# A fifth chunk of seven-product blocks in a down projection, with a last stage that works by pairs of tiles

## The chip, the cores and the metric

The kernel runs on one core of a Trainium2 chip. The metric is the device time of one execution in microseconds (us); the median of three runs before the change is 2358.19 us (2357.68 to 2359.34). PE is TensorE (matrix products), DVE VectorE, ACT ScalarE, POOL GpSimd, SP SyncE, whose queue issues most transfers.

## The reference, cut to what matters

One encoder layer: a layer norm, a token mixer (a recurrence and an attention), a second norm, a gated feed-forward network with a short convolution, and a third norm. There are 544 tokens: 512 of a prompt and 32 of a running stream. The change lies in the last two lines, the down projection and the norm behind it.

```python
D_MODEL = 2048
D_FF = 5632
...
def conv_ffn(x, conv_buf, w_up, w_gate, conv_w, conv_b, w_down):
    T = x.shape[1]
    u = x @ w_up
    ext = jnp.concatenate([conv_buf.astype(u.dtype), u], axis=1)
    a = conv_b + sum(ext[:, j:j + T] * conv_w[j] for j in range(CONV_W))
    h = jax.nn.silu(a) * (x @ w_gate)
    return h @ w_down, ext[:, -(CONV_W - 1):]
...
        ff, conv_new = conv_ffn(h, conv_cache[l], w_ffn_up[l], w_ffn_gate[l], conv_w[l], conv_b[l], w_ffn_down[l])
        h = layer_norm(ALPHA * h + ff, ln2_g[l], ln2_b[l])
```

## The kernel before

Features lie on the 128 partitions, tokens along the free axis, in two halves of NI = 272 tokens (`H_[0]`, the first tokens, and `H_[1]`, the second). Every operand of a matmul is held as a rounded high part and a remainder, the low part, and each product is taken three times: high by high, high by low, low by high. A weight block of 128 x 1024 is loaded by SP into one of eight raw slots (`pump` takes the next of `pending` whenever a slot comes free; `release` frees one), ACT rounds it into `wh` (L1193) and DVE takes the remainder into `wl` (L1194). There are three buffers for each.

**Block products.** The up, gate and down projections use a scheme with seven products in place of eight for a 2 x 2 split of K, outputs and tokens. The products are named 11, s1, s2, s4, s3, 12, 22 (`ORDER`); s1, s2, s3 and 22 need a difference of weight blocks, which DVE forms in place (`Blocks.form`, L1186). One `Item` or `Twin` is one product: 24 matmuls of 128 x 272 into one PSUM bank. X banks take 11 and add s2, s3 and 22 to it; B banks take s1 and s4, and then 12. After each product `sink` adds a bank to the sum `y` in SBUF. `PLACE` says which quarter of y a product's bank belongs to: (output tile of a pair, half of the tokens). So s4 and 12 reach the first tokens only.

**Order.** `play` (from L1585) writes the engines' order out by hand. While PE multiplies item n, DVE adds the bank of item n-1, DVE and ACT split the weight of item n+2 (`prep`), and DVE forms the weight of item n+3. Smaller tasks wait in `fills`, each with a cost, and `drain` takes them in the room that an item leaves. `hooks` put transfers and other work behind named items. All of PE, DVE and ACT keep the order of the program.

**Down projection.** `CHUNKS` of four pairs of hidden tiles each go through block products: four chunks, 16 pairs, 32 K tiles (FD). A chunk has four rounds, one for each quarter q of the output tiles, and each round has the seven products. The operands of a chunk (sums and differences of hidden tiles, in two parts) are made in the up and gate stage (`gated`, from L1511: four sums and two `part`s for each pair below NS) and go through DRAM (`op_dr`). Of the pairs from NS on, `hid_dr` takes the plain hidden tiles.

**The K tiles that are left.** Twelve K tiles in three groups of four are taken plainly, by 8 pairs of output tiles c: `Whole` items for both halves of the tokens at once, one group for c = 4 to 7 and two for c = 0 to 3; then `last_half(1)` and `last_half(0)` take the rest for the second and the first tokens, pair by pair in the order `LAST`. `before_last` takes the second last group for c = 4 to 7, `last` the last one for all. In each half `Norm.first` finds a rough mean from the first pair, which is taken off everything that follows (`cb`): by GpSimd in the second tokens (`collect`, L2095), by a matmul in the first (`shift`, L2083). ACT squares each tile, DVE and GpSimd add up the sums s1 and s2. `Norm.stats` brings them across the partitions by matmuls, GpSimd takes the power -1/2, matmuls spread mean and scale. The second tokens are normalised tile by tile while the first tokens' products run (`scaled_last`, L2046 and L2047), and the first tokens at the very end (L2168, L2170, L2191 on DVE, L1133 and L1134 on GpSimd, L2037 on ACT), each tile stored by a transfer of its own (L2038).

Of the kernel before, what the change touches and what calls it, by code (L numbers as in the profile page):

```python
# [15 lines left out]
P = 128  # L16
D = 2048
# [30 lines left out]
CHUNKS = (4, 4, 4, 4)  # L48
# [11 lines left out]
def tile_encoder_step(ctx, tc, xp, xs, w_in, w_in4, w_kr, w_q_b, w_kv_b, w_out, w_up, w_gate, w_down, w_down2,  # L60
# [1560 lines left out]
    with tc.manual_schedule():  # L1621
# [190 lines left out]

        def down_items(g, q):
# [11 lines left out]
            def sink(name, x):  # L1825
                t, j = PLACE[name]
                ps = twin(banks[x])
                y = ysq[q].rearrange("p (c t) n -> p c t n", c=2)[:, :, t, H_[j]]
                if g == 0 and (t, j) not in fresh:
                    fresh.add((t, j))  # L1830
                    V.scalar_tensor_tensor(out=y, in0=y, scalar=ALPHA, in1=ps, op0=ALU.mult, op1=ALU.add)
                else:
                    V.tensor_tensor(out=y, in0=y, in1=ps, op=ALU.add)
# [9 lines left out]
        class Whole:  # L1843

            n, name = 8, "11"

            def __init__(self, c, g, tiles, first, last):
                self.c, self.k0, self.tiles, self.first, self.last = c, FD + 4 * g, tiles, first, last
                self.g, self.raw, self.time, self.sink = self, {}, 6.0, self.gather if last else None
                pending.append((self, "11", w_down2[g, c], 8))  # L1850

            def form(self):
                return 0.0

            def prep(self):
                self.w = [t.rearrange("p (k c) -> p k c", k=4) for t in rounded(self.raw["11"].t, 8)]
                release(self, "11")
                return 1.25

            def multiply(self):  # L1860
                if self.first:
                    self.tiles += [main_tile(), psA.tile([P, 1024], F32, name="acc", tag="acc")]
                for t in range(2):
                    for k in range(4):
                        mm3(both(self.tiles[t]), (self.w[0][:, k], self.w[1][:, k]), (t * P, t * P + P),
                            hid[self.k0 + k], self.first and k == 0, self.last and k == 3)

            def gather(self):
                for t in range(2):
                    y = ysq[self.c // 2][:, 2 * (self.c % 2) + t]  # L1870
                    V.tensor_tensor(out=y, in0=y, in1=hold(self.tiles[t]), op=ALU.add)
                return 1.5
# [6 lines left out]
        NG = (NF - FD) // 4  # L1879
        for c in (4, 5, 6, 7, 0, 1, 2, 3):  # L1880
            tiles, gs = [], range(NG - 2 if c >= 4 else NG - 1)
            items += [Whole(c, g, tiles, g == 0, g == gs[-1]) for g in gs]

# [11 lines left out]
        staged = {}  # L1895

        def stage_hid(g, name):
            t = staged[g] = home[name].tile([P, 4, T], F32, name=f"hx{g}", tag=f"op{name}0")
            G.dma_start(t, hid_dr[:, 4 * g:4 * g + 4])

        def split_group(g, i):
            for b, name in enumerate(("11", "12")):
                t = home[name].tile([P, 2, 2, T], R, name=f"hid{name}", tag=f"op{name}{i}")
                for f in range(2):
                    split_hid(FD + 4 * g + 2 * b + f, staged[g][:, 2 * b + f], t[:, f, 0], t[:, f, 1])
# [10 lines left out]
        L4 = (NW - NU) // len(CHUNKS)  # L1916
# [3 lines left out]
        n3 = NU + 3 * L4  # L1920
        at(n3 + 2, lambda: stage_hid(0, "s1"))
        at(n3 + 5, lambda: split_group(0, 0))
        at(n3 + 10, lambda: stage_hid(1, "s2"))
        at(NW, lambda: split_group(1, 1))
        at(NW - 8, lambda: retired.add(lt))

        ws9, ws10, tail = {}, {}, {}
# [5 lines left out]

        late9 = {c: Late(w_down2[NG - 2, c]) for c in (4,)}
        late10 = {c: Late(w_down2[NG - 1, c]) for c in (4, 5)}
        late9.update({c: Late(w_down2[NG - 2, c]) for c in range(5, 8)})

        def open_tail():
            x1_stack.close()
            free[:] = [s for s in free if s[0] is not lt]  # L1940
            tail["ap"] = ctx.enter_context(pool("ap2", bufs=KD))
            tail["hp2"] = ctx.enter_context(pool("hp2", "right"))
            tail["sps"], sp = stack(pool("sp", "right"))
            tail["hx"] = sp.tile([P, 4, T], F32, name="hx")
            G.dma_start(tail["hx"], hid_dr[:, 4 * NG - 4:])

        def split_tail_hid():
            for f in range(4):
                h, l = (tail["hp2"].tile([P, T], R, name=f"h{n}{f}") for n in "HL")
                split_hid(NF - 4 + f, tail["hx"][:, f], h, l)  # L1950

        def split_10(c, src):
            rv = src.rearrange("p (k c) -> p k c", k=4)
            for t in range(2):
                wh, wl = (tail["ap"].tile([P, 512], R, name=n, tag=n).rearrange("p (k c) -> p k c", k=4)
                          for n in ("aH", "aL"))
                A.activation(wh, rv[:, :, t * P:(t + 1) * P], AF.Copy)
                V.tensor_tensor(out=wl, in0=rv[:, :, t * P:(t + 1) * P], in1=wh.bitcast(F32), op=ALU.subtract)
                ws10[2 * c + t] = wh, wl

        def first_10(c):
            split_10(c, late10[c].raw["w"].t)
            release(late10[c], "w")

        def split_9(c):
            src = late9[c].raw["w"].t
            if c == 4:
                w = [p.tile([P, 8 * P], R, name=tag, tag=tag) for p, tag in (free.pop() for _ in range(2))]
                A.activation(w[0], src, AF.Copy)
                V.tensor_tensor(out=w[1], in0=src, in1=w[0].bitcast(F32), op=ALU.subtract)  # L1970
            else:
                w = rounded(src, 8)
            ws9[c] = [t.rearrange("p (k c) -> p k c", k=4) for t in w]
            release(late9[c], "w")

        at(NW + 3, open_tail)
        at(NW + 5, split_tail_hid)
        at(NW + 8, lambda: first_10(4))
        at(NW + 9, lambda: first_10(5))
        at(NW + 9, lambda: split_9(4))  # L1980
        at(NW + 10, lambda: split_9(5))
        at(NW + 11, lambda: split_9(6))

# [5 lines left out]
        split_9(7)  # L1989
        dma(conv_d, uc)  # L1990
        ys = [ysq[k // 4][:, k % 4] for k in range(KD)]
        tail["sps"].close()


    with pool("tl") as ff:
        LAST = (4, 5, 6, 0, 1, 2, 3, 7)

        def split_last(c):
            p, tag = free.pop(0)
            free.append((p, tag))  # L2000
            t = p.tile([P, 8 * P], F32, name=tag, tag=tag)
            dma(t, w_down2[NG - 1, c])
            split_10(c, t)

        split_last(6)
        split_last(0)
# [10 lines left out]

        turn = [0]

        def tail_tag(name):  # L2020
            turn[0] += 1
            return ("a", "ext")[turn[0] % 2], 2

        one_f = ff.tile([P, P], F32, name="one_f", tag="ext", bufs=2)
        ones_r = ff.tile([P, P], R, name="ones_r")
        V.memset(one_f, 1.0)
        A.activation(ones_r, one_f, AF.Copy)
        nrms = {j: Norm(ff, j, tail_tag) for j in range(2)}
        queue = []

        def out_a(k, j, eng):
            nrms[j].scale(ys[k], eng, eng)

        def out_b(k, j, eng=A):
            z = ys[k][:, H_[j]]
            if eng:
                eng.activation(z, z, AF.Identity, bias=col(C_LN2_B + k), scale=col(C_LN2_G + k))  # L2037
            dma(y_d[k * P:(k + 1) * P, H_[j]], z)  # L2038

        OUT_AT = {1: (0, 4), 2: (4, 6), 3: (6, 8), 4: (8, 10), 5: (10, 12), 6: (12, 14), 7: (14, 15)}  # L2040

        def scaled_last(i, ks=None):
            ks = ks or range(*OUT_AT[i])
            for k in ks:
                z = ys[k][:, H_[1]]
                V.tensor_tensor(out=z, in0=z, in1=nrms[1].mups, op=ALU.subtract)  # L2046
                V.tensor_tensor(out=z, in0=z, in1=nrms[1].rsps, op=ALU.mult)  # L2047
            for k in ks:
                out_b(k, 1)

        def held_stats(nrm):
            for _ in range(3):
                yield
            ps = acc_tile()
# [242 lines left out]
```

## Time and profile before

| what | value |
|---|---|
| median of three runs | 2358.19 us (2357.68 to 2359.34) |
| the profiled execution | 2358.93 us, its span 2357.2 us |
| granted clock of PE, mean | 0.994 |
| instructions | 44395 |
| block products of the down projection, last matmul | from 1849.8 to 2186.5 us |

The profiler records one execution. The page first gives the busy time of every engine, with the share of the span and the count of instructions, and the span in 40 equal slices. A view of windows gives busy time and counts by stretch. A time line has start, duration, engine, line, operation, output <- inputs, shapes, count and, in brackets, how long the engine stood before it and what released it. Groups have busy time, mean ns of one, then idle time before. Times are from the start of the span. Matmuls overlap: a duration of one is longer than the pitch from one to the next.

### The profile page before, as it was taken

What the parts mean: (1) busy time and instruction counts of PE and PEld (TensorE: products, weight loads), DVE (VectorE), ACT (ScalarE), POOL (GpSimd) and SP (SyncE); (2) the same over time, 40 slices, a digit from 0 to 9 for tenths busy, and PEclk for the clock granted to TensorE, in tenths of its full rate; (3) what the DMA queues carried; (4) which work ended last, traced back from release to release, by engine and by line L of the source; (5) the groups of instructions that cost most, each with busy time, mean ns of one, the idle gap of its engine ahead of it and who ended that gap; (6) DMA issues with size and microseconds to landing.
All of it is one profiled execution on the core that took longest, in us unless ns stands there. A gap on an engine that the chain in (4) does not pass through costs nothing.

```text
span 2357.2 us, 44395 instructions
## 1 busy us (share of the span) xinstructions
PE 2317.3 (98%) x18430; PEld 2302.0 (98%) x18430; DVE 1798.8 (76%) x2483; ACT 1064.4 (45%) x1654; POOL 121.9 (5%) x167
## 2 busy tenths in 40 slices
PE   7999999999999999999999999999999999999997
PEld 6999999999999999999999999999999999999997
DVE  6455578777786358989888888888777888888566
ACT  5345434434452237655554555545444433333234
POOL 1010000000001111000000000000000100000023
PEclk9999999999999999999999999999999999999998
DMA  6332263322245236534435344353334973643322
GB/s 238 102 100 83 69 208 99 91 88 80 80 152 193 87 111 220 182 130 159 170 112 192 117 157 158 114 189 118 127 118 141 367 291 106 233 146 93 109 71 77
DMA packets 129129, 334.53 MB, mean 142 GB/s; under 512 B 12064, under 2 KB 60960, under 8 KB 124320
## 3 DMA queue, kind: packets, MB, share of 16 engines
q1 hardware_dynamic: 122096, 286.01, 36.8%
q0 software_dynamic: 6832, 45.68, 4.9%
q8 instruction: 145, 2.38, 0.4%
q14 instruction: 56, 0.46, 0.1%
HBM read 272.78 MB, written 56.15 MB: 140 GB/s over the span
## 4 chain that ended last, share of the span: by engine, by line
PE 93%; DVE 3%; DMA 1%; ACT 1%; issue 1%; POOL 0%; ACTq 0%; SPq 0%; DVEq 0%
PE main L1248 21%; PE acc L1248 16%; PE main L118 16%; PE main L788 11%; PE main L1279 8%; PE acc L1279 6%; PE acc L118 6%; PE s L853 2%; PE main L555 1%; PE at L616 1%; PE at L585 1%; DMA x<-in_xp 1%; DVE wl L1194 1%; PE main L542 0%; DMA raw<-in_w_in 0%
## 5 line engine op out<-in xcount | busy, mean ns | idle before, releaser
L1193 ACT ACTIVATE wh<-raw 128x1024 fp32r<-128x1024 f32 x347 | 367.4, 1060 | 433.5 <-DVE raw L1186 132.4
L1194 DVE TENSOR_TENSOR wl<-raw,wh 128x1024 fp32r<-128x1024 f32 x347 | 424.3, 1223 | 131.5 <-ACT wh L1193 130.5
L1248 PE MATMUL main<-op,wh 128*128 128x272 f32 x1408 | 265.5, 287 | 0.0
L1248 PE MATMUL acc<-ops,wh 128*128 128x272 f32 x1344 | 254.2, 287 | 0.0
L1248 PE MATMUL main<-ops,wh 128*128 128x272 f32 x1344 | 254.2, 287 | 0.0
L1248 PEld LDWEIGHTS main<-op,wh 128*128 128x128 f32 x1408 | 221.0, 188 | 0.0
L1248 PEld LDWEIGHTS acc<-ops,wh 128*128 128x128 f32 x1344 | 211.0, 188 | 0.0
L1248 PEld LDWEIGHTS main<-ops,wh 128*128 128x128 f32 x1344 | 211.0, 188 | 0.0
L1248 PE MATMUL main<-op,wl 128*128 128x272 f32 x704 | 203.0, 288 | 0.3 <-DVE wl L1194 0.3
L1248 PE MATMUL acc<-ops,wl 128*128 128x272 f32 x672 | 193.8, 288 | 0.0
L1248 PE MATMUL main<-ops,wl 128*128 128x272 f32 x672 | 193.7, 288 | 0.0
L118 PE MATMUL main<-aH,wh 128*128 128x272 f32 (+2 forms) x736 | 176.5, 296 | 0.2 <-ACT wh L280 0.2
L118 PE MATMUL main<-aH,wl 128*128 128x272 f32 (+2 forms) x736 | 172.9, 292 | 1.8 <-DVE wl L281 1.8
L118 PE MATMUL main<-aL,wh 128*128 128x272 f32 (+2 forms) x736 | 172.3, 291 | 1.0 <-DVE aL L269 1.0
L1248 PE MATMUL acc<-op,wh 128*128 128x272 f32 x832 | 159.0, 289 | 3.5 <-DVE eg L1475 3.5
L107 DVE TENSOR_TENSOR wl<-raw,wh 128x1024 fp32r<-128x1024 f32 (+2 forms) x72 | 80.2, 1117 | 89.8 <-ACT wh L106 85.7
L1186 DVE TENSOR_TENSOR raw<-raw,raw 128x1024 f32<-128x1024 f32 x114 | 139.4, 1223 | 2.7
L732 ACT ACTIVATE wh<-raw 128x1024 fp32r<-128x1024 f32 x84 | 88.7, 1056 | 111.4 <-DVE raw L727 105.1
L1248 PEld LDWEIGHTS acc<-op,wh 128*128 128x128 f32 x832 | 131.7, 190 | 3.7 <-issue 3.7
L1248 PEld LDWEIGHTS main<-op,wl 128*128 128x128 f32 x704 | 132.2, 188 | 0.5 <-DVE wl L1194 0.5
L1194 DVE TENSOR_TENSOR wl<-rawl,wh 128x1024 fp32r<-128x1024 f32 x86 | 105.2, 1223 | 31.3 <-ACT wh L1193 31.3
L1193 ACT ACTIVATE wh<-rawl 128x1024 fp32r<-128x1024 f32 x86 | 91.0, 1058 | 82.7 <-DVE rawl L1186 42.4
(435 smaller groups left out, 6078.1 us busy)
## 6 DMA issues: line engine op xcount, KB each, us to landing
raw<-in_w_in SPq DMA_DIRECT2D x76, 512.0 KB, 3.6
raw<-in_w_up SPq DMA_DIRECT2D x72, 512.0 KB, 4.3
raw<-in_w_gate SPq DMA_DIRECT2D x72, 512.0 KB, 4.3
raw<-in_w_down SPq DMA_DIRECT2D x70, 512.0 KB, 3.8
raw<-in_w_out SPq DMA_DIRECT2D x40, 512.0 KB, 3.5
opd<-ohl SPq DMA_DIRECT2D x16, 1088.0 KB, 5.5
ops<-opd POOLq DMA_DIRECT2D x16, 1088.0 KB, 9.7
opd<-ohl SPq DMA_DIRECT2D x16, 816.0 KB, 6.7
```

The lines of the kernel that those rows point to most:

```text
L107: V.tensor_tensor(out=dst(lv), in0=src(rv), in1=dst(hv).bitcast(F32), op=ALU.subtract)
L118: PE.matmul(ps, ww[:, wcols[0]:wcols[1]], aa[:, hs[j]], start=first and i == 0, stop=last and i == 2, skip_group_check=True)
L555: PE.matmul(ps[:, j * 512:j * 512 + 256], l[k][:, a:b], r4(w[:, k:k + 1, :])[:, 0, :, 128:256], start=k == 0 and i == 0, stop=k == 1 and i ...
L585: PE.matmul(sc[:, :nk], qn[j][:, q0:q0 + P], kn[j][:, :nk], start=True, stop=False)
L732: A.activation(wh, self.src, AF.Copy)
L788: PE.matmul(out, ww[:, k * P:(k + 1) * P], aa, start=name in ("11", "s1", "12") and k == 0 and q == 0, stop=k == HK - 1 and q == 2, skip_g ...
L853: PE.matmul(ps[:, j * 64:(j + 1) * 64], Kp[:, a:b], Qv[:, j * bt:(j + 1) * bt, 1, :], start=True, stop=True)
L1186: V.tensor_tensor(out=out, in0=a, in1=b, op=ALU.subtract)
L1193: A.activation(wh, src, AF.Copy)
L1194: V.tensor_tensor(out=wl, in0=src, in1=wh.bitcast(F32), op=ALU.subtract)
L1248: PE.matmul(ps, ww[:, k * P:(k + 1) * P], aa, start=self.first and k == 0 and i == 0, stop=k == n - 1 and i == 2, skip_group_check=True)
L1279: PE.matmul(banks[:, 512 * u:512 * u + NI], ww[:, (u * n + k) * P:(u * n + k + 1) * P], aa, start=self.first and k == 0 and i == 0, stop=k ...
```

## The change

A fifth chunk joins the block products: 20 pairs, 40 K tiles, so only four K tiles are left for the plain last stage. Pairs 16 to 19 now make operands in the up and gate stage. The `Whole` items and `before_last` go.

In the fifth chunk (g == SPLIT) the rounds have only 11, s1, s2, s3 and 22 (`FIRST`). As there is no s4 between them, the bank of s1 is added twice, to the place of s1 and to that of s4. The weights of s4 and 12 are loaded anew (`own_half`), and their eight products (`half_products`) stand between `last_half(1)` and `last_half(0)`, as they reach the first tokens only.

The last stage works by pairs of tiles: adds, squares, sums and normalisation take 544 columns at once. The second tokens' rough mean is now taken off by matmuls as well; the sums of a pair are folded at the end (`fold_both`); the first two pairs are recentred at pair 3; the weights of the last K tiles are split by `split_tail`, four of them at the last items of the fifth chunk and four in `last_half(1)`, which also splits the first two of the eight weights (`half_prep`). The second tokens are normalised during the eight products (`norm_first`), two pairs of them by GpSimd. At the end the first tokens' mean comes from one matmul with a matrix of 1/D, and a pair is stored by one transfer; the output in DRAM has a layout by halves and pairs, which the host undoes.

```diff
-CHUNKS = (4, 4, 4, 4)
+CHUNKS = (4, 4, 4, 4, 4)
...
+        SPLIT = len(CHUNKS) - 1
+        FIRST = ("11", "s1", "s2", "s3", "22")
+
+        def add_part(q, name, ps):
+            t, j = PLACE[name]
+            y = ysq[q].rearrange("p (c t) n -> p c t n", c=2)[:, :, t, H_[j]]
+            V.tensor_tensor(out=y, in0=y, in1=ps, op=ALU.add)
...
+                if g == SPLIT and name == "s1":
+                    add_part(q, "s4", ps)
                 return 0.75
...
-            for name in ORDER:
+            for name in (ORDER if g < SPLIT else FIRST):
...
+        def split_tail(i):
+            c = LAST[i]
+            src = late[c].raw["w"].t
...
+            A.activation(wh, src, AF.Copy)
+            V.tensor_tensor(out=wl, in0=src, in1=wh.bitcast(F32), op=ALU.subtract)
+            release(late[c], "w")
...
+        n4 = NU + SPLIT * L4
+        at(n4 + 2, stage_hid)
+        at(n4 + 5, split_last_hid)
+        for i in range(4):
+            at(NW - 4 + i, lambda i=i: split_tail(i))
...
+        late = {c: Late(w_down2[0, c]) for c in LAST}
+        own_half = [(q, name, Late(w_down[q, a, b, :, 8 * SPLIT * P:8 * (SPLIT + 1) * P]))
+                    for q in (2, 3, 0, 1) for name, a, b in (("s4", 1, 1), ("12", 1, 0))]
...
+            def recentre(self, c):
+                V.scalar_tensor_tensor(out=self.y(c), in0=wide2(self.cb.bitcast(F32)), scalar=float(P), in1=self.y(c),
+                                       op0=ALU.mult, op1=ALU.add)
+
+            def collect(self, c):
+                e = fresh()
+                A.activation(e, self.y(c), AF.Square)
+                self.held.append((c, e))
...
+                V.tensor_tensor(out=self.s1w, in0=self.y(b) if n == 2 else self.s1w, in1=self.y(c), op=ALU.add)
...
+                    V.tensor_tensor(out=self.s2w, in0=self.s2w, in1=e, op=ALU.add)
...
+        NORM_V = {2: 0, 3: 1, 4: 2, 5: 3, 6: 4, 7: 7}
+        NORM_G = {2: 6, 4: 5}
+
+        def norm_first(n):
+            n1 = nrms[1]
+            if n in NORM_G:
+                less(NORM_G[n], 1, n1.mub, G)
+                times(NORM_G[n], 1, n1.rsb, G)
+            if n in NORM_V:
+                less(NORM_V[n], 1, n1.mups)
+                times(NORM_V[n], 1, n1.rsps)
+                out_pair(NORM_V[n], 1)
+            if n - 2 in NORM_G:
+                out_pair(NORM_G[n - 2], 1)
...
+        def half_products():
+            prev = None
+            for n, (q, name, _) in enumerate(own_half):
+                ps = acc_tile()
+                wh, wl = half_w.pop(n)
...
+                    if u == 0:
+                        if prev:
+                            add_part(*prev)
+                        half_prep(n + 2)
+                        norm_first(n)
+                    yield
+                    pump()
+                prev = q, name, twin(ps)
+            add_part(*prev)
...
+                if i > 3:
+                    add_y(b)
+                    nrm.collect(b)
+                    if final:
+                        nrm.fold_both()
                 last(c, 0)
                 yield
+                if i == 1:
+                    add_y(b)
+                    queue.append(nrm.start(b))
                 if i == 2:
...
                     add_y(b)
...
+                if i == 3:
+                    for n in range(2):
+                        nrm.recentre(LAST[n])
+                        nrm.collect(LAST[n])
+                    add_y(b)
+                    nrm.collect(b)
...
                 last(c, 1)
                 yield
...
+                if 1 < i and not final:
                     shift(c)
...
+                if j and i < 4:
+                    split_tail(4 + i)
+                    pump()
+                if j and i > 5:
+                    half_prep(i - 6)
...
+            if j:
+                add_y(c)
+                nrm.collect(c)
+                nrm.fold_both()
+                queue.append(first_stats(nrm))
...
+        for _ in (s for part in (last_half(1), half_products(), last_half(0)) for s in part):
+            for chain in queue:
+                next(chain, None)
...
-_OUTS = [("y", (D, T)), ("lat", (256, T)), ("kr", (64, T)), ("stp", (HEADS, P, P)), ("sts", (HEADS, P, P)),
+_OUTS = [("y", (2, HK, P, T)), ("lat", (256, T)), ("kr", (64, T)), ("stp", (HEADS, P, P)), ("sts", (HEADS, P, P)),
```

`first_stats` takes one step for each step of the products: nothing at first, then the sums s1 and s2 across the partitions on PE and the row factors, nothing, then the spreads.

More of the change, by code (lines that the diff above doesn't have):

```diff
@@ L1841, in down_items @@
             return out
[L1843 to L1872, printed above, removed]
         NU = len(items)
@@ L1961, in first_10 @@
[L1961 to L1974, printed above, removed]
@@ L2040, in tile_encoder_step @@
[L2040 to L2054, printed above, removed]
-            held.add(id(ps))
-            yield from nrm.stats(ps=ps)
+            return edge[turn[0] % 2][:, 6:8]
@@ new lines, in tile_encoder_step, with less, times, out_pair @@
+        nrms = {j: Edge(j) for j in range(2)}
+        queue = []
+        def less(c, j, mu, eng=V):
+            eng.tensor_tensor(out=ypair(c, j), in0=ypair(c, j), in1=wide2(mu), op=ALU.subtract)
+        def times(c, j, rs, eng=V):
+            eng.tensor_tensor(out=ypair(c, j), in0=ypair(c, j), in1=wide2(rs), op=ALU.mult)
+        def out_pair(c, j, own=()):
+            for k in (2 * c, 2 * c + 1):
+                if k not in own:
+                    z = ys[k][:, H_[j]]
+                    A.activation(z, z, AF.Identity, bias=col(C_LN2_B + k), scale=col(C_LN2_G + k))
+            dma(y_d[j, c].rearrange("p (t n) -> p t n", t=2), ypair(c, j))
@@ new lines, in first_stats @@
+        def first_stats(nrm):
+            yield
+            ps = nrm.ps = acc_tile()
+            held.add(id(ps))
+            row_stats(nrm, ps)
+            dm, rs = row_factor(nrm, ps)
+            yield
+            yield
+            nrm.mups, nrm.rsps = ps[:, 16:16 + NI], ps[:, 512:512 + NI]
+            nrm.spread(nrm.mups, dm)
+            nrm.spread(nrm.rsps, rs)
+            nrm.mub, nrm.rsb = nrm.keep("n_mu"), nrm.keep("n_rs")
+            A.activation(nrm.mub, nrm.mups, AF.Copy)
+            A.activation(nrm.rsb, nrm.rsps, AF.Copy)
@@ new lines, in tile_encoder_step @@
+        for _ in (s for part in (last_half(1), half_products(), last_half(0)) for s in part):
+            for chain in queue:
+                next(chain, None)
+        nrm = nrms[0]
+        mean_w = mean_ws[0]
+        mu, rsb = nrm.keep("n_mu"), nrm.keep("n_rs")
+        ps, mups = acc_tile(), nrms[1].ps[:, :NI]
+        on_g, mixed = (2, 6), 4
+        on_v = [c for c in range(8) if c not in (*on_g, mixed)]
+        nrm.sums(ps, nrm.s1)
+        PE.matmul(mups, mean_w, nrm.s1, start=True, stop=True)
@@ new lines, in tile_encoder_step @@
+        nrm.sums(ps[:, 4:], nrm.s2)
+        less(on_v[0], 0, mups)
+        _, rs = row_factor(nrm, ps)
+        for c in on_v[1:3]:
+            less(c, 0, mups)
+        A.activation(mu, mups, AF.Copy)
+        rsps = acc_tile()[:, :NI]
+        nrm.spread(rsps, rs)
+        A.activation(rsb, rsps, AF.Copy)
+        for c in on_g:
+            less(c, 0, mu, G)
+            times(c, 0, rsb, G)
+        z = [ys[2 * mixed + t][:, nrm.cols] for t in range(2)]
+        G.tensor_tensor(out=z[0], in0=z[0], in1=mu, op=ALU.subtract)
```

316 lines of the change are left out of this document (132 added, 184 removed).

## The prediction

> **What bounds the kernel now.** I read the page's shares and slices first, then the windows of the last 505 us, then the time lines of VectorE and ScalarE inside one round of block products, and last the end of the program.
>
> ```profile
> PE 2317.3 (98%) x18430; PEld 2302.0 (98%) x18430; DVE 1798.8 (76%) x2483; ACT 1064.4 (45%) x1654; POOL 121.9 (5%) x167
> PEclk9999999999999999999999999999999999999998
> ```
> ```profile
> 1600.00:1700.00 100.00, 100.00 (x800) 100.00 (x800) 82.18 (x86) 50.10 (x77) 0.00 (x0) 1.00 0.36 120
> 1700.00:1800.00 100.00, 100.00 (x800) 100.00 (x799) 75.54 (x75) 47.91 (x73) 0.00 (x0) 1.00 0.39 122
> 1852.00:2190.00 338.00, 337.88 (x2697) 337.68 (x2696) 289.53 (x296) 123.38 (x123) 13.31 (x25) 1.00 0.53 193
> 2190.00:2338.00 148.00, 148.00 (x1189) 147.96 (x1187) 91.36 (x170) 50.27 (x87) 23.40 (x29) 1.00 0.23 72
> ```
>
> The columns are the stretch, its length, then busy time and count of PE, PEld, DVE, ACT and POOL, then the clock and the DMA share. PE has no gap: the kernel is a string of matmuls. DVE is 86% busy (289.5 of 338) while block products run, and only 62% (91.4 of 148) in the last 148 us, where eight K tiles are taken plainly. The change moves work from the second kind of stage into the first.
>
> The pace of PE comes from the chain, where 22 and the next round's 11 are one piece of 48 matmuls:
>
> ```profile
> 2057.54 6.01 PE main L1279 x48
> 2078.59 6.01 PE main L1279 x48
> ```
> ```profile
> L1279 PE MATMUL main<-op,wl x256: 286/288/291, 1849.8 to 2186.5; 128*128 128x272 f32 x128
> ```
>
> One matmul takes 6.01/48 = 0.125 us of PE (its 288 ns overlap the next two), a product of 24 takes 3.006, a round of seven 21.05. The block products end at about 2186.7. Now DVE and ACT in that same round:
>
> ```profile
> 2077.89 1.22 DVE L1186 TENSOR_TENSOR raw<-raw,raw 128x1024 f32<-128x1024 f32 x1
> 2079.04 0.71 DVE L1833 TENSOR_TENSOR y<-y,acc 128x544 f32<-128x544 f32 x1
> 2080.33 1.23 DVE L1194 TENSOR_TENSOR wl<-raw,wh 128x1024 fp32r<-128x1024 f32 x1 [0.58 <-ACT wh L1193]
> 2081.59 1.23 DVE L1186 TENSOR_TENSOR raw<-raw,raw 128x1024 f32<-128x1024 f32 x1
> 2082.73 0.71 DVE L1833 TENSOR_TENSOR y<-y,main 128x544 f32<-128x544 f32 x1
> 2084.02 1.23 DVE L1194 TENSOR_TENSOR wl<-raw,wh 128x1024 fp32r<-128x1024 f32 x1 [0.57 <-ACT wh L1193]
> 2085.16 0.72 DVE L1833 TENSOR_TENSOR y<-y,main 128x544 f32<-128x544 f32 x1
> 2085.79 1.22 DVE L1194 TENSOR_TENSOR wl<-raw,wh 128x1024 fp32r<-128x1024 f32 x1
> 2086.93 1.22 DVE L1186 TENSOR_TENSOR raw<-raw,raw 128x1024 f32<-128x1024 f32 x1
> 2088.06 0.72 DVE L1833 TENSOR_TENSOR y<-y,acc 128x544 f32<-128x544 f32 x1
> ```
> ```profile
> 2079.23 1.06 ACT L1193 ACTIVATE wh<-raw 128x1024 fp32r<-128x1024 f32 x1 [2.63 <-DVE raw L1186]
> 2082.93 1.06 ACT L1193 ACTIVATE wh<-raw 128x1024 fp32r<-128x1024 f32 x1 [2.63 <-DVE raw L1186]
> ```
>
> For each product DVE adds a result to y (L1833), makes the low part of a weight two products ahead (L1194), and for four of the seven forms a weight difference three ahead (L1186). A formed weight goes DVE, ACT (`wh`, 1.06 us), DVE, so DVE stands 0.58 us at the low part however late it is. From one add to the next, three kinds of step follow: wait and form 3.69 us (2079.04 to 2082.73), wait alone 2.43 (to 2085.16), form alone 2.90 (to 2088.06). In the order 11, s1, s2, s4, s3, 12, 22 the seven steps need 3 x 2.43 + 3 x 2.90 + 3.69 = 19.68 us. PE needs 21.05, so DVE has 1.37 to spare, and PE never waits.
>
> **The change, part by part.**
>
> *Matmuls.* Out go 16 output tiles x 8 K tiles x 3 x 2 = 768 plain matmuls; in come 4 x 7 products x 24 = 672. That is 96 x 0.125 = **-12.0 us**. Both halves now shift by PE, 12 matmuls each, in place of these 14: 10 x 0.125 = **+1.2**. The small sums and spreads stay the same in number.
>
> ```profile
> L2083 PE MATMUL main<-n_cb,ones_r 128*128 128x272 f32 x11 | 2.3, 287 | 0.0
> L2083 PE MATMUL acc<-n_cb,ones_r 128*128 128x272 f32 x3 | 0.7, 287 | 0.0
> ```
>
> *Up and gate stage.* Pairs 16 to 19 now form operands. That stage shows its price: 82 us of DVE in 100 where pairs form them, 75.5 where they don't, PE full in both. Cost 0; the cover is 18 us of idle DVE per 100. Their stores and loads replace part of the hidden store's and keep the same queues; SP's next weights have whole rounds to land. The y layout touches only SP's last DMAs.
>
> *Chunk 5.* Its rounds are 11, s1, s2, s3, 22: five products, 15.03 us of PE, but all four formed weights and six adds, since s1 is added twice. Steps: 11, s1 and 22 are wait and form, 3 x 3.69; s2 is 2.43, its second add lying where the wait was; s3 is 2.90. Together 16.40. DVE now lacks 1.37 us a round, 5.5 in four rounds. The low parts of the last four hidden tiles (0.72 us each by the row below, 0.63 when back to back) add 2.5. The last round drops two low parts and two forms of a round to come and takes four `split_tail` instead, the same time, but two of these stand ahead of the low part of 22: 0.4. DVE's lead is worth some 2.5: its low part must be ready 6.0 us after its step's start by PE, and is now ready 3.5 after (add 1.13 late, 1.29 to the low part, 1.22). Stall **+5.9**.
>
> ```profile
> L1893 DVE TENSOR_TENSOR hid<-hx,hid x8: 718/719/720, 2124.8 to 2213.0; 128x544 fp32r<-128x544 f32 x8
> ```
>
> *Second tokens' last K tiles (`last_half(1)`).* Per pair PE takes 24 matmuls and two shifts, 3.26 us.
>
> ```profile
> 2314.62 0.74 PE L1053 MATMUL acc<-ident,nt_c 128*128 128x128 f32 x6
> 2316.78 0.41 PE L2083 MATMUL main<-n_cb,ones_r 128*128 128x272 f32 x2
> ```
> ```profile
> 2315.39 0.40 ACT L1073 ACTIVATE n_cb<-acc 128x272 fp32r<-128x272 f32 x1 [1.38 <-PE acc L1053]
> 2316.29 0.43 ACT L1083 ACTIVATE n_e<-y 128x272 f32<-128x272 f32 x1 [0.51 <-DVE y L1079]
> ```
>
> Before, a stretch of matmuls stood between the spread and the first shift; now pair 2's shift follows the spread at once, so PE waits for ACT's 0.40 plus signals: +0.55 in each half. On ACT the round of pair 6's weight (1.06) is queued behind that `cb`, so DVE is free only 2.05 after pair 3 starts (0.2 less from `cb`, 1.06, 1.22). Pair 3 then asks for two recentrings, three adds and two sums of squares (7 x 0.63), three waits of 0.3 for ACT's squares and a split of 1.26: 6.6 us. DVE is 2.05 + 6.6 - 3.26 = 5.4 behind PE at pair 4. Pairs 4 and 5 cost 2.25 and win 1.0 each; 6 and 7 each carry a `half_prep`, 3.5, so DVE is 4 behind when pair 7 ends. Then come its add, squares and folds, 3.0. `first_stats` sets its sums on PE after the first block product, 3.0 after that end, and they need what is ready at 7: PE stands, and the products behind stand with it. With 0.25 for the first half weight: **+4.6** with the first half's `cb` wait.
>
> *The eight products between the halves.* Each costs PE 3.0 and DVE an add 0.63, a low part 1.26, and for n of 2 to 7 two passes over a pair 2 x 0.63. That sum is near PE's, but the engines are in one loop: the next rounding on ACT is queued behind this product's two output activations, and these wait for DVE's passes.
>
> ```profile
> L2037 ACT ACTIVATE y<-y,par x29: 597/614/618, 2310.9 to 2353.1; 128x272 f32<-128x272 f32 x29
> ```
>
> One turn is low part 1.26, passes 1.27, output 2 x 0.57 (6 took 3.40 in the row of ACT below) and rounding 1.06, with signals 4.9 us; after n = 4 two more outputs, 6.0. From n = 2 the low parts of 4, 5, 6, 7 end at about 2.0, 6.9, 11.8 and 17.8 us, with the last one an estimate that could gain a microsecond by overlap; PE wants them 6, 9, 12 and 15 after. **+3.4.**
>
> *First tokens' last K tiles.* DVE needs 2.25 per pair of 3.26: only the second `cb` wait, **+0.55**.
>
> *The end.*
>
> ```profile
> 2338.21 0.44 DVE L2090 TENSOR_TENSOR y<-y,acc 128x272 f32<-128x272 f32 x1
> 2339.18 1.50 PE L1048 MATMUL main<-ones,n_s 128*128 128x1 f32 x12 [1.00 <-DVE n_s L2099]
> 2343.25 1.48 DVE L2168 TENSOR_TENSOR y<-y,main 128x272 f32<-128x272 f32 x4 [1.98 <-ACT n_mu L1122]
> 2344.65 0.43 DVE L2170 TENSOR_TENSOR y<-y,main 128x272 f32<-128x272 f32 x1
> 2345.11 3.40 ACT L2037 ACTIVATE y<-y,par 128x272 f32<-128x272 f32 x6 [0.62 <-DVE y L2170]
> 2352.58 1.12 ACT L2037 ACTIVATE y<-y,par 128x272 f32<-128x272 f32 x2 [0.35 <-DVE y L2170]
> ```
>
> The mean comes straight from one matmul, so subtraction starts some 2 us sooner; but the scale still waits for sums, power and spread, and the multiplication starts no sooner than 6.3 us after the last add, as now (2344.65 against 2338.21). Then ACT has 14 activations x 0.57 = 8.0, where the span from 2345.11 to the end at 2353.70 is 8.6: -0.6. Against that, the two folds stand ahead of the last adds, about +0.9, and the last DMA moves a pair. A one-row full-precision matmul over 272 columns isn't in the trace; below it bounds six spread matmuls, 0.74, above two such sets, 1.5, and it delays the second sums by that. I take 1.0, nearest the spread. End: **+0.6**, from -1 to +2.
>
> *Sum:* -12.0 + 1.2 + 5.9 + 4.6 + 3.4 + 0.55 + 0.6 = +4.25 on the profiled 2358.93 us (its span is 2357.2, with 1.7 around it): 2363.2. The median shown is 0.74 lower, so **2362.4 us**, +0.18%. A run of this kernel can tell about 0.2%, 4.7 us, from no change.
>
> **Rivals.**
>
> *PE stays the bound everywhere.* The waits at `wh` vanish once DVE is late, and nothing stalls. For it: PE is at 100% now with DVE at 86%. Against: DVE was already 1.13 us late at 2082.73 and still stood 0.57 at the next low part. It gives -12.0 + 1.2 + 0.6: 2348.
>
> *Half the stalls.* DVE comes out of pair 3 almost on time, because ACT's rounding of pair 6's weight gets ahead of the `cb`, or because recentring overlaps; then the sums stall 0.5, not 3.8, and the output loop starts with a lead. Chunk 5 keeps its 5.9. That is 6 us less: 2356.
>
> *Slower, by the lock of GpSimd.* In the middle products GpSimd normalises two pairs in four passes. What such company costs is in the trace:
>
> ```profile
> L1099 DVE TENSOR_TENSOR n_s<-n_s,n_e 128x272 f32<-128x272 f32 x28 | 15.6, 558 | 0.7
> 2286.22 0.88 DVE L2104 TENSOR_TENSOR n_s<-n_s,y 128x272 f32<-128x272 f32 x1
> 2287.02 1.00 DVE L1099 TENSOR_TENSOR n_s<-n_s,n_e 128x272 f32<-128x272 f32 x1
> 2287.95 0.43 DVE L2104 TENSOR_TENSOR n_s<-n_s,y 128x272 f32<-128x272 f32 x1
> 2286.03 1.70 POOL L2095 TENSOR_TENSOR y<-y,n_cb 128x272 f32<-128x272 f32 x2 [1.43 <-DVE y L2090]
> ```
>
> While GpSimd ran (2286.03 to 2287.73) the same DVE add took 0.88 and 1.00, after it 0.43. A pass over a pair is 1.5 to 1.7 there, so each low part it meets is held for up to that long; two or three of the four passes meet one, +4, all of it inside the loop that is already too long. It decides when a low part starts after a GpSimd pass has begun. With it the time is 2366.5 to 2370. [...]
>
> **How the numbers follow.** Forecast 0.50 (2358 to 2366: within 0.2% of the median 0.30, slower 0.20); PE the bound 0.13 (faster); half the stalls 0.22 (faster 0.10, within 0.12); the lock 0.15 (slower). So faster 0.23, same 0.42, slower 0.35. The range leaves out the first rival (0.13) and the far end of the last: 2349.5 to 2370, which also takes in the end's -1 to +2 and a lead between 1 and 4.
>
> **What would show it.** In the changed kernel PE's product pitch in chunk 5 should be 3.0 at first and 3.2 to 3.6 from its second round on; PE should stand about 4 us ahead of the sums after the first of the eight products, waiting for a fold on DVE, and again ahead of the last two, waiting for their low parts; two waits of half a microsecond belong to `cb`. If the rounds run at 15.0 with no gap, the first rival holds; if only chunk 5 has gaps, the second. I'd be wrong from the ground up if a DMA were what PE waits for.

## The result and the profile after

| kernel | median, us | lowest to highest | profiled execution, its span | granted clock |
|---|---|---|---|---|
| before | 2358.59 (4 runs, taken beside those of after) | 2357.68 to 2359.34 | 2358.93, 2357.2 | 0.994 |
| after | 2381.20 (4 runs) | 2380.86 to 2382.37 | 2380.86, 2379.1 | 0.989 |

The changed kernel is **0.97% slower**: after over before is 1.0097, with a 95% interval from 1.0079 to 1.0114. That lies above the predicted range. The likeliest single time, 2362.4, lay on the right side, but only as far off as a run can tell from no change: of some 22 us, the forecast had 4.

The page's row of engines and the windows answer to those shown of before (columns as there); the last window is that of chunk 5:

```profile
PE 2318.0 (97%) x18340; PEld 2299.9 (97%) x18340; DVE 1843.3 (77%) x2485; ACT 1074.4 (45%) x1652; POOL 107.6 (5%) x145
```
```profile
1600.00:1700.00 100.00, 100.00 (x801) 100.00 (x800) 87.20 (x99) 54.09 (x85) 0.00 (x0) 1.00 0.38 127
1852.00:2190.00 338.00, 337.86 (x2699) 337.67 (x2698) 289.72 (x294) 120.39 (x118) 15.90 (x30) 1.00 0.57 208
2186.50:2266.50 80.00, 66.24 (x481) 64.65 (x481) 61.94 (x66) 24.94 (x26) 0.00 (x0) 0.94 0.41 128
```

The operands of pairs 16 to 19 cost nothing: DVE rises to 87 us of 100, and PE stays full. The four old chunks run as before. The loss stands in the last row. Chunk 5 takes 80 us, of which PE is busy for 66, and its clock is 0.94. PE's waits from 2184 us on say for what it stands (engine and line, released by, then us in total, times, longest):

```profile
PE main L1279 <- DVE y L1841: 10.4, 6, 3.4
PE main L1279 <- issue: 3.4, 2, 2.5
PE main L1048 <- DVE edge L2013: 2.7, 1, 2.7
...
PE acc L2067 <- ACT wh L1193: 1.5, 1, 1.5
PE acc L2067 <- DVE wl L1194: 1.2, 2, 0.7
PE main L2090 <- ACT rt L1991: 0.5, 1, 0.5
```

The first two rows, 13.8 us together, are eight waits in chunk 5. What PE waits for is not a low part (L1194) but the add of a result to y (L1841), and the bank is always `main`, the X bank. The chain of chunk 5 shows one round at a time: a gap, s3, a gap, 22 (start, us, what):

```profile
2197.90 4.70 PE main L1279 x24
2202.61 0.86 issue
2203.47 3.12 PE main L1279 x23
...
2218.14 3.25 PE main L1279 x24
2236.36 4.79 PE main L1279 x24
...
2257.73 4.57 PE main L1279 x24
...
2266.43 3.02 PE main L118 x24
```

Two things are new here: the gaps ahead of s3 and of 22, and a product s3 that takes 4.6 to 4.8 us in three rounds of four, though a product is 3.0. What PE and DVE did around the first gap stands in their time lines (start, us, line, operation, output <- inputs):

```profile
2195.10 0.28 PE L1279 MATMUL main<-ops,wl 128*128 128x272 f32 x1
2197.90 0.49 PE L1279 MATMUL main<-ops,wh 128*128 128x272 f32 x2 [2.52 <-issue]
```
```profile
2195.29 0.72 DVE L1819 TENSOR_TENSOR y<-y,acc 128x544 f32<-128x544 f32 x1
2195.95 1.23 DVE L1194 TENSOR_TENSOR wl<-raw,wh 128x1024 fp32r<-128x1024 f32 x1
2197.09 0.71 DVE L1841 TENSOR_TENSOR y<-y,main 128x544 f32<-128x544 f32 x1
...
2202.64 0.72 DVE L1841 TENSOR_TENSOR y<-y,main 128x544 f32<-128x544 f32 x1 [2.45 <-PE main L1279]
```

PE set out on the last matmul of s2 at 2195.10 and then stood 2.52 us. DVE added s1 for the second time (L1819) and then made a low part; only at 2197.09 did it add the X bank with s2 in it. That add ended at 2197.80, and s3 started at 2197.90. The add behind s3 was not late at all: DVE stood 2.45 us for it, started at 2202.64 as s3 ended, and PE still waited 0.86, because 22 goes on adding to that bank only after the add has read it: the add ended at 2203.36, and 22 started at 2203.47.

**The reason** is the order of banks. 11 starts an X bank, and s2, s3 and 22 accumulate in it, each state of it being added to another quarter of y. In the order of seven, 11, s1, s2, s4, s3, 12, 22, a B product lies ahead of every one of them, so the add has a product's time. With s4 and 12 taken out, s2, s3 and 22 follow each other, and PE and DVE take turns at one bank.

### The profile page after: what moved, and what is told of

It is laid out like the page before. It is cut to its first block, busy times and chain, and to the rows that moved or that the text cites. A ratio compares the mean times of both kernels' runs of the same rounds, so it can differ in the third digit from the quotient of the medians.

```text
span 2379.1 us, 44175 instructions
## 1 busy us (share of the span) xinstructions
PE 2318.0 (97%) x18340; PEld 2299.9 (97%) x18340; DVE 1843.3 (77%) x2485; ACT 1074.4 (45%) x1652; POOL 107.6 (5%) x145
## 4 chain that ended last, share of the span: by engine, by line
PE 90%; DVE 5%; ACT 2%; issue 1%; DMA 0%; POOL 0%; SPq 0%; ACTq 0%; DVEq 0%
PE main L1248 21%; PE acc L1248 16%; PE main L118 13%; PE main L788 11%; PE main L1279 9%; PE acc L1279 6%; PE acc L118 4%; PE s L853 2%; DVE wl L1194 1%; ACT wh L1193 1%; PE main L555 1%; PE at L616 1%; PE at L585 1%; DVE raw L1186 1%; PE main L542 0%
## 5 line engine op out<-in xcount | busy, mean ns | idle before, releaser
L1193 ACT ACTIVATE wh<-raw 128x1024 fp32r<-128x1024 f32 x355 | 375.5, 1059 | 425.4 <-DVE raw L1186 150.8
L1194 DVE TENSOR_TENSOR wl<-raw,wh 128x1024 fp32r<-128x1024 f32 x355 | 434.6, 1224 | 120.4 <-ACT wh L1193 120.1
L1248 PE MATMUL main<-ops,wh 128*128 128x272 f32 x1344 | 254.1, 287 | 0.0
L1186 DVE TENSOR_TENSOR raw<-raw,raw 128x1024 f32<-128x1024 f32 x123 | 150.5, 1223 | 2.8
L732 ACT ACTIVATE wh<-raw 128x1024 fp32r<-128x1024 f32 x84 | 88.7, 1055 | 111.4 <-DVE raw L727 105.1
L1193 ACT ACTIVATE wh<-rawl 128x1024 fp32r<-128x1024 f32 x91 | 96.6, 1061 | 91.1 <-DVE rawl L1186 47.7
L1279 PE MATMUL main<-ops,wh 128*128 128x272 f32 x640 | 125.9, 294 | 10.2 <-DVE y L1841 7.7
L1194 DVE TENSOR_TENSOR wl<-rawl,wh 128x1024 fp32r<-128x1024 f32 x91 | 111.3, 1223 | 29.2 <-ACT wh L1193 29.2
```

Of the source, the lines that this page charges most:

```text
L732: A.activation(wh, self.src, AF.Copy)
L1186: V.tensor_tensor(out=out, in0=a, in1=b, op=ALU.subtract)
L1193: A.activation(wh, src, AF.Copy)
L1194: V.tensor_tensor(out=wl, in0=src, in1=wh.bitcast(F32), op=ALU.subtract)
L1248: PE.matmul(ps, ww[:, k * P:(k + 1) * P], aa, start=self.first and k == 0 and i == 0, stop=k == n - 1 and i == 2, skip_group_check=True)
L1279: PE.matmul(banks[:, 512 * u:512 * u + NI], ww[:, (u * n + k) * P:(u * n + k + 1) * P], aa, start=self.first and k == 0 and i == 0, stop=k ...
```

## The experiments

A second measure is used beside the medians: the time from the first block product of the down projection to the end of the span, in the profiled executions. The first block product starts between 1847.1 and 1849.7 us in all these runs (at 1849.5 in before), and what lies ahead of that is the same program in after and the variants, so this measure leaves out a drift of up to 2.6 us that has nothing to do with the edits. Where the intervals of two ratios overlap, as from one version to the next in the last three rows, the medians alone don't tell the two apart, and what an edit did is read from the traces.

| kernel | median, us | ratio to before, 95% interval | from first block product to end |
|---|---|---|---|
| before | 2358.06 to 2358.82 | 1 | 507.7 |
| after | 2381.20 | 1.0097 (1.0079 to 1.0114) | 529.9 |
| e1_other_bank | 2364.57 | 1.0027 (1.0017 to 1.0036) | 515.5 |
| e2_warm | 2376.79 | 1.0077 (1.0060 to 1.0094) | 525.3 |
| e3_seven | 2355.93 | 0.9990 (0.9980 to 0.9999) | 505.4 |
| e4_out_later | 2373.60 | 1.0062 (1.0047 to 1.0077) | 523.4 |
| e6_sums_later | 2377.02 | 1.0082 (1.0068 to 1.0096) | 527.5 |
| e5_seven_late_norm | 2352.14 | 0.9974 (0.9965 to 0.9984) | 502.4 |
| e7_copy_first | 2350.36 | 0.9966 (0.9954 to 0.9979) | 501.1 |
| e8_warm_end | 2350.97 | 0.9968 (0.9956 to 0.9981) | 501.1 |

### Is it the bank?

In chunk 5 the adds behind s2 and s3 read the bank of s1, so these two states of the X bank never reach y, and y is another sum than the layer's. All instructions, sizes and loads stay; only the turn-taking at the X bank goes for these two.

```diff
             def sink(name, x):
                 t, j = PLACE[name]
-                ps = twin(banks[x])
+                ps = twin(banks[x and not (g == SPLIT and name in ("s2", "s3"))])
```

> In the fifth chunk the adds that follow s2 and s3 read the bank of s1 instead of the bank that PE goes on with (so y is another sum; DVE has the same work). If PE waits because s3 and 22 go on in a bank that DVE has not yet read (the bank theory), the gaps of 13.8 us ahead of s3 and 22 go, what is left is the stall of late weight parts that I had predicted, and the fifth chunk takes 62 to 67 us in place of 80.0: 2363 to 2368 us. If PE waits because DVE as a whole is late (the rival), the chunk stays at 78 to 80: 2379 to 2382 us.

Measured: 2364.57 us (2363.23 to 2366.43), 16.6 less than after; from the first block product on it is 14.4. Waits, PE's time line at both of them, and the chain of the chunk:

```profile
PE main L1279 <- DVE y L1841: 3.1, 2, 2.3
```
```profile
2207.11 0.49 PE L1279 MATMUL main<-ops,wh 128*128 128x272 f32 x2 [0.83 <-DVE y L1841]
...
2224.64 0.79 PE L1279 MATMUL main<-ops,wh 128*128 128x272 f32 x2 [2.27 <-DVE y L1841]
```
```profile
2224.64 13.79 PE main L1279 x96
```

Eight waits of 13.8 us become two of 3.1, and s2, s3, 22 and the next 11 run as one piece (96 matmuls). The chunk takes 65.7 us, from 2185.25 to 2250.98, 14.3 less than in after; that much was the turn-taking at the bank with what followed from it. Twenty products of 3.006 are 60.1, so 5.6 us of stall are left. The prediction had 5.9 for DVE's load, but the nearness is partly luck. The two waits are not for low parts: s2 waits for the late add behind 11. And of the 5.6 about 1.8 is slow matmuls, since the 96 take 13.79 us in place of 12.0; the chunk's clock is 0.97.

### Is the slow product a matter of the clock?

A window of after, laid around the s3 behind the first gap, shows the granted clock in the third column from the end:

```profile
2197.80:2202.70 4.90, 4.70 (x24) 4.41 (x24) 2.42 (x4) 0.23 (x1) 0.00 (x0) 0.65 0.42 139
```

In that s3 it is 0.65; in 22, from 2203.40 to 2206.60, it is 1.00 again. If the gap itself lowers the clock, filling it with matmuls should bring the pace back though the gap stays: 18 of them ahead of s3 and 5 ahead of 22, into a bank that nobody reads.

```diff
...
+            def keep_busy(it, spare):
+                if not spare:
+                    spare.append(psA.tile([P, 1024], F32, name="acc", tag="acc"))
+                for _ in range(18 if it.name == "s3" else 5):
+                    PE.matmul(spare[0][:, :NI], it.w[0][:, :P], it.ops["11"][0][:, 0, 0], start=True, stop=True,
+                              skip_group_check=True)
...
+                if g == SPLIT and name in ("s3", "22"):
+                    out[-1].idle = lambda it: keep_busy(it, spare)
```

> The changed kernel with 18 extra matmuls ahead of s3 and 5 ahead of 22 in the fifth chunk, into a bank that nobody reads, so that PE is busy in the gaps (2.25 and 0.6 us of work). If the products after a gap take 4.6 us in place of 3.0 because the clock was lowered in the gap (clock theory), they take 3.0 again: 4 to 5 us less, 2376 to 2377 us, and the granted clock of the chunk is 1.0 in place of 0.94. If they are slow for another reason, the time stays at 2381 or rises by up to 3.

Measured: 2376.79 us (2376.35 to 2377.11), 4.4 less than after; the intervals of the two ratios overlap, but the time from the first block product falls by as much, 529.9 to 525.3. The window of the chunk:

```profile
2186.50:2262.00 75.50, 73.26 (x574) 71.75 (x573) 61.92 (x65) 24.98 (x26) 0.00 (x0) 1.00 0.43 137
```

The clock is 1.00, and the chunk ends 4.5 us sooner with 92 matmuls more in it. Its gaps are filled, not gone. So of the 20 us that the chunk takes beyond its products, about 14 are waits at the bank and about 5 are the clock (0.94 in after).

### Without the split order: seven products in chunk 5 too

The fifth chunk stays, but takes the order of seven, and the eight products between the halves go. The second tokens are then normalised in the first tokens' stage.

```diff
-        FIRST = ("11", "s1", "s2", "s3", "22")
+        FIRST = ORDER
...
-                if g == SPLIT and name == "s1":
-                    add_part(q, "s4", ps)
...
-        own_half = [(q, name, Late(w_down[q, a, b, :, 8 * SPLIT * P:8 * (SPLIT + 1) * P]))
-                    for q in (2, 3, 0, 1) for name, a, b in (("s4", 1, 1), ("12", 1, 0))]
+        own_half = []
...
-        NORM_V = {2: 0, 3: 1, 4: 2, 5: 3, 6: 4, 7: 7}
-        NORM_G = {2: 6, 4: 5}
+        NORM_V = {1: (0,), 2: (1, 7), 4: (2,), 5: (3,), 6: (4,)}
+        NORM_G = {1: 6, 3: 5}
...
+                if not j:
+                    norm_first(i)
```

> The fifth chunk with all seven products in the order of the other chunks, none left between the halves; the second tokens are normalised during the first tokens' last K tiles, and the sums come half a product later. Bank theory: s1, s4 and 12 lie between the products of the X bank, so the chunk takes 84.2 us with no gap (21.05 a round); with 10.8 us of matmuls saved and 3 to 6 us of waits in the last stage: 2350 to 2356 us. Rival (a fifth chunk is too much for DVE in whatever order): the rounds take over 22 us, and the time is over 2362.

Measured: 2355.93 us (2354.49 to 2356.85). The chunk, then PE's longest wait behind it:

```profile
2186.50:2271.00 84.50, 84.50 (x677) 84.50 (x676) 74.45 (x79) 33.59 (x34) 0.20 (x1) 1.00 0.32 102
```
```profile
PE main L1048 <- DVE edges L2099: 5.8, 1, 5.8
```

The chunk with all seven products has no gap at all. It takes 84.1 us (2186.65 to 2270.78), 4.1 more than the chunk of five products in after, and the eight products, with their waits, are gone from the stage behind. What is late next is DVE at the end: PE stands 5.8 us for the first tokens' sums, because the normalisation of the second tokens lies ahead of them on DVE.

### The eight products: whose loop is it?

The output activations of a pair are moved one product later, behind the rounding of the next weight on ACT. GpSimd's passes stay as they are.

```diff
             if n in NORM_V:
                 less(NORM_V[n], 1, n1.mups)
                 times(NORM_V[n], 1, n1.rsps)
-                out_pair(NORM_V[n], 1)
+            if n - 1 in NORM_V:
+                out_pair(NORM_V[n - 1], 1)
...
+            out_pair(NORM_V[7], 1)
```

> The changed kernel with the output activations of a pair one product later in the middle stage, behind the next rounding on ACT. If the loop of rounding, low part, passes and activations holds PE there, the waits of 0.5, 1.5 and 0.7 us and the slow product behind them (1.5) go: 3 to 4 us less, 2377 to 2378 us. If DVE's own work or the lock by GpSimd holds it, under 1 us changes.

Measured: 2373.60 us (2372.36 to 2374.07), 7.6 less than after, about twice what was expected. The chain from the second to the last of the eight products:

```profile
2305.06 3.10 PE main L2068 x24
2308.16 6.01 PE acc L2068 x48
2314.17 3.00 PE main L2068 x24
2317.17 6.01 PE acc L2068 x48
```

No wait is left, where after had 0.5, 1.5 and 0.7. So the loop of ACT's outputs and roundings made them, as predicted, and not GpSimd's passes, which are all still there. The profiled executions differ by 8.5 us, of which 2.0 lie ahead of the first block product (1847.2 against 1849.2) and are no work of this edit. Behind that point it is 6.5: the waits of 2.7, the slow product behind them (4.46 in after, 1.45 over a product) and 1.5 at the end, where the first six sums took 0.83 us in place of 1.37, by luck, as shown below; 0.8 stays unassigned.

### The sums of the second tokens half a product later

```diff
         def first_stats(nrm):
...
+            yield
...
-            yield
```

> The changed kernel with the sums of the second tokens half a product later on PE (12 matmuls, 1.5 us). If PE waits there only because DVE's folds come 2.7 us after PE is ready, the wait falls to about 1.2, and the product behind it runs at full pace again since the gap is short (4.6 to 3.0): 2 to 3 us less, 2378 to 2379 us. If the wait only moves on to the spread and the passes behind it, under 1 us changes.

Measured: 2377.02 us (2375.89 to 2380.16), 4.2 less than after, with overlapping intervals; from the first block product 2.4 less. The chain there:

```profile
2299.49 2.35 PE main L2067 x12
```

The wait falls from 2.66 to 0.97. The product beside it still runs slower: its half of 12 matmuls takes 2.35 where 1.5 would do, and from 2300.06 on a lone matmul in it lasts 0.42 to 0.43 us in place of 0.29. The expectation had full pace there because the gap is short; that failed.

### The version that beats both

e3_seven with three edits: pairs 2, 3 and 4 of the second tokens are normalised at the very end, while PE forms the last sums; the last mean gets a bank of its own, so that the second tokens' mean stays where it is; the first shift of each half comes a stretch later, so that PE doesn't stand for `cb`.

```diff
-        NORM_V = {1: (0,), 2: (1, 7), 4: (2,), 5: (3,), 6: (4,)}
+        NORM_V = {1: (0,), 2: (1, 7)}
...
+                    shift(b)
...
-                if 1 < i and not final:
+                if 2 < i and not final:
...
-        ps, mups = acc_tile(), nrms[1].ps[:, :NI]
+        ps = acc_tile()
+        mups = ps[:, 512:512 + NI]
...
+        for c in (2, 3):
+            norm_one(c)
...
+        norm_one(4)
```

> The run with all seven products, with three of the second tokens' pairs normalised only while PE forms the first tokens' sums at the end, and with the first shift of each half one stretch of matmuls later. In the run before, PE stood 5.8 us behind the last matmul for DVE's sums. If that is DVE being late by the normalisation between, the wait falls to 2 to 3.5 us, and 2 x 0.5 us of waits for the rough mean go: 2351 to 2353 us. If the late passes only move to the end and lengthen it, 2355 to 2357 us.

Measured: 2352.14 us (2351.11 to 2353.27). The two longest waits of PE behind chunk 5:

```profile
PE main L1053 <- POOL nt_rs L2168: 2.2, 1, 2.2
PE main L1048 <- DVE edges L2102: 1.9, 1, 1.9
```

The 5.8 of e3_seven are 1.9, and the two waits of 0.5 for `cb` are gone; one wait of PE for an add in the first tokens' stage, 0.9 in e3_seven, is 1.5 here. But the multiplication at the end came late by ACT, which stood in pair 4's outputs when the scale was ready to be copied (DVE's time line, 1.47 for the copy at L2209):

```profile
2338.16 1.99 DVE L2023 TENSOR_TENSOR y<-y,main 128x544 f32<-128x544 f32 x3 [1.47 <-ACT edges L2209]
```

The next kernel puts these outputs behind the copy:

```diff
-        norm_one(4)
+        less(4, 1, nrms[1].mups)
+        times(4, 1, nrms[1].rsps)
...
+        out_pair(4, 1)
```

> The version with all seven products and three late normalisations (2352.1 us), with the output activations of pair 4 behind ACT's copy of the scale. DVE's first multiplication by the scale came 0.4 us after that copy, and the copy was held by the two activations for 1.2 us. If the multiplication waits for the copy, 0.8 to 1.2 us less: 2351 us. If it waits for the spread alone, no change.

Measured: 2350.36 us (2349.95 to 2351.34), beside 2358.82 for before: a ratio of 0.9966 (0.9954 to 0.9979). From the first block product it is 1.3 less than e5_seven_late_norm; some 0.4 of that is no work of the edit, since the first six sums took 1.29 there and 0.83 here, behind a wait of 1.94 in both. A last kernel keeps PE busy around the final sums, with 15 and 16 spare matmuls:

```diff
+                keep_busy(15)
...
+        keep_busy(16)
```

> The kernel of e7_copy_first with 15 extra matmuls behind the last shift and 16 behind the last sums, into a bank that nobody reads. If the clock falls in the two waits of 1.9 and 2.2 us there, the sums (1.3 us for six), the mean (1.25 for two) and the spread (1.5) run at 0.7, 0.6 and 0.7 again: 1.5 to 2.5 us less than e7_copy_first. If their pace comes from something else, no change, or up to 0.5 us more where the extra matmuls outlast a wait.

Measured: 2350.97 us (2349.86 to 2351.76), no gain. The six spread matmuls in e7_copy_first and in e8_warm_end, and in the latter the step of DVE that starts the row factor:

```profile
2328.99 0.83 PE L1048 MATMUL main<-ones,edges 128*128 128x1 f32 x6 [1.94 <-DVE edges L2102]
...
2334.30 1.46 PE L1053 MATMUL main<-ident,nt_rs 128*128 128x128 f32 x6 [3.36 <-POOL nt_rs L2168]
```
```profile
2333.89 0.84 PE L1053 MATMUL main<-ident,nt_rs 128*128 128x128 f32 x6 [1.19 <-POOL nt_rs L2177]
```
```profile
2332.36 0.15 DVE L2174 TENSOR_SCALAR nt_dm<-main 128x3 f32<-128x3 f32 x1
```

The spread is faster, 0.84 for 1.46, but it starts no sooner, 486.8 us after the first block product in both: the sums had run at full pace in e7_copy_first already (0.83), and DVE, busy with the late normalisation, comes to the row factor only at 2332.36. From the first block product to the end both take 501.1, so PE's pace isn't what ends last there.

## Why the prediction was wrong, point by point

- **Matmuls, -12.0 + 1.2: held.** Where nothing waits, a product of after takes 3.0 us as before. The last 148 us of before hold all twelve plain K tiles, and not eight; the sum rightly moves eight of them.
- **Up and gate stage, 0: held**, at a DVE load of 87% where PE still has no gap.
- **Chunk 5, +5.9: this step failed.** From 2186.36 to 2266.43 the chunk takes 80.07 us, 19.95 above its twenty products. The step counted DVE's work in a round of five, 16.40 us, and that count was right: in e1_other_bank, where DVE never stands for a product of PE, the adds behind 11 in the first two rounds start 16.30 apart (2189.96 and 2206.26). What failed is the path from there to PE. The step let PE wait only for a late low part, and took the add of a bank as work that only has to be done some time within the round. No wait of PE in chunk 5 is for a low part. Between s2, s3 and 22 the add is a link in PE's own chain: 0.86 to 0.91 us at 22, where DVE was on time, and 1.8 to 3.4 at s3, where it was late. The section on the kernel before says that X banks take 11 and add the others to it, but the step never asked which product now follows which in that bank. No rival covered it either. The signs named for the rounds failed with it: they take 18.8 to 21.2 us from the first one on, 3.8 to 4.2 a product, where 3.0 and then 3.2 to 3.6 were foreseen.
- **The clock: not in the prediction at all.** The four s3 take 4.70, 3.25, 4.79 and 4.57 us, 5.3 together above 4 x 3.006, at granted clocks of 0.65, 1.00, 0.65 and 0.68 in the windows around them; e2_warm wins 4.4 to 4.6 of that back.
- **Second tokens' stage, +4.6 with the first `cb` wait: right in size (4.8), partly by luck.** `cb` costs 0.49 (0.55 foreseen). The sums wait 2.66 rather than 3.8, for a fold on DVE as foreseen, but the product behind them takes 4.63, 1.6 of it the clock (granted 0.63 in it), which the prediction didn't have.
- **Eight products, +3.4: right mechanism.** Waits of 0.49, 1.48 and 0.74 make 2.7, and the last product runs 1.45 longer by the clock (granted 0.63 from 2325.69 to 2330.00): 4.2. The rival on GpSimd's passes falls, since e4_out_later keeps these passes and loses the waits. That a low part is held for up to a pass of 1.5 to 1.7 us, +4 in all, was the author's estimate, and no run shows it. Two low parts of after started while such a pass ran: the one at 2308.79 took 1.26 us (pass until 2308.97), the one at 2313.57 took 1.56 (pass until 2314.05), where the others of that stage take 1.22 to 1.23: 0.3, and not 4. "PE stays the bound" and "half the stalls" fall with chunk 5.
- **Second `cb` wait, +0.55: held**, 0.49.
- **End, +0.6: too small, +2.5.** From the last shift's end to the span's end it is 21.5 us (2357.57 to 2379.1), and was 19.0 (2338.18 to 2357.2). These rows of after carry it:

```profile
2358.57 0.43 DVE L2098 TENSOR_TENSOR y<-y,main 128x272 f32<-128x272 f32 x1
```
```profile
2359.53 1.37 PE L1048 MATMUL acc<-ones,edges 128*128 128x1 f32 x6 [1.96 <-DVE edges L2101]
2360.76 1.25 PE L2192 MATMUL main<-edges,mean_w 128*128 128x272 f32 x2
```
```profile
2366.59 1.98 DVE L2026 TENSOR_TENSOR y<-y,acc 128x544 f32<-128x544 f32 x3 [1.65 <-ACT edges L2201]
```

The last add is 1.0 late by the folds (0.9 foreseen). From it to the multiplication it is 8.0, where before had 6.4; the forecast allowed 6.3 at the least and 1.0 for the matmul of the mean. The 0.6 that the activations should have won didn't come: 12.5 us from the multiplication to the end, as before. In e4_out_later the same groups ran at full pace:

```profile
2352.56 0.83 PE L1048 MATMUL acc<-ones,edges 128*128 128x1 f32 x6 [1.95 <-DVE edges L2103]
2353.25 0.70 PE L2194 MATMUL main<-edges,mean_w 128*128 128x272 f32 x2
```

and its end took 20.0 us: 1.5 of the 2.5 is the clock again, which in after was 0.54 over the first six sums and 0.50 over the mean.

Added up: -10.8 + 19.95 + 0.49 + (2.66 + 1.62) + 4.15 + 0.49 + 2.5 = +21.1 where the profiled executions differ by 22.2 from the first block product on; 1.1 isn't assigned. Of the 21.1, chunk 5's excess over its step is 14, and everything else together is 3 above the forecast.

## What to carry to other kernels

Before products are taken out of a hand-written order, write down which PSUM bank each one uses and who reads that bank between two of them: a product that looks like work only may be the room in which an add is hidden. Stalls on PE of 1.8 to 3.4 us cost 0.2 to 1.8 more in the product behind them here, so price them with the clock, or fill them with matmuls nobody reads (4.5 us of chunk 5 in e2_warm). Here the plainer version, the full order of seven and no extra stage, had neither a gap nor a fall of the clock in chunk 5 (84.50 us of PE in 84.50, granted 1.00).

## What the runs showed of the hardware that was not expected

**In these runs the length of a gap alone didn't decide whether the clock fell.** In after the gap of 2.52 us ahead of the first s3 was followed by a product of 4.70 us at a granted clock of 0.65, the one of 2.42 ahead of the second s3 by one of 3.25 at 1.00. In e6_sums_later, with the same two gaps, it was the other way round (granted 1.00 from 2195.90 to 2201.00, and 0.79 from 2216.10 to 2221.00):

```profile
2196.01 0.49 PE L1279 MATMUL main<-ops,wh 128*128 128x272 f32 x2 [2.53 <-issue]
...
2214.80 0.79 PE L1279 MATMUL main<-ops,wh 128*128 128x272 f32 x2 [2.42 <-DVE y L1841]
```
```profile
2196.01 3.25 PE main L1279 x24
...
2214.80 4.75 PE main L1279 x24
```

The time line of after shows where the pace changes within a product; a lone matmul (x1) lasts 0.28 us at full pace and 0.43 at the lower one, two in one row (x2) 0.41 and 0.65, and rows in between mark the change:

```profile
2198.98 0.29 PE L1279 MATMUL main<-ops,wl 128*128 128x272 f32 x1
...
2236.70 0.36 PE L1279 MATMUL main<-ops,wl 128*128 128x272 f32 x1
...
2240.03 0.36 PE L1279 MATMUL main<-ops,wl 128*128 128x272 f32 x1
...
2260.59 0.45 PE L1279 MATMUL main<-ops,wh 128*128 128x272 f32 x2
...
2304.85 0.50 PE L2067 MATMUL acc<-op,wh 128*128 128x272 f32 x2
...
2328.80 0.47 PE L2067 MATMUL acc<-op,wh 128*128 128x272 f32 x2
```

Behind the first gap the pace falls only after 2198.98, 1.1 us after PE went on at 2197.90. One slow stretch is seen whole, from 2236.70 to 2240.03: 3.3 us at a granted clock of 0.51, in which a matmul takes 0.227 us of PE (3 in 0.68, from 2237.31 to 2237.99) and not 0.125. The rows at 2260.59, 2304.85 and 2328.80 are the ends of three others. What decides whether the clock falls was not settled. The gap ahead of the third s3 of after was 1.83 us, and a slow product followed (4.79 us, granted 0.65), while behind the second gap of 2.42 the clock stayed at 1.00; and in e6_sums_later a gap of 0.97, with twelve matmuls of one column (1.50 us) behind it, was followed by the lower pace.

**The full-precision matmul of the mean over 272 columns** (with a matrix of 128 x 128 and not, as the prediction has it, one row) went as two instructions and took 0.70 us in e4_out_later and 1.25 in after, where the granted clock was 0.50 (lines 2194 and 2192 in the rows above); the prediction could only bound it, between 0.74 and 1.5.
